# Which expert down products are computed during routing, and where the row steps stand beside them

## The chip, the core and the metric

The kernel runs on one core of a Trainium2 chip. The metric is device time in microseconds (us), the median of several runs. The core has a matrix engine (TensorE, PE in the profile; its weight loads are PEld), VectorE (DVE), ScalarE (ACT), GpSimd (POOL) and SyncE (SP), each with a queue of its own that is worked off in order, and 16 DMA engines that all queues share.

## What is computed

One layer of a trunk: a mixer of three branches, and then an expert layer (PEER) that takes most of the time. 512 tokens, width 2048, all in float32. The part that this case turns on:

```python
def peer_retrieve(h, w_q, sub_keys):                 # 8 heads, 2 x 128 keys, top 16
    q = (h @ w_q).reshape(t, PEER_HEADS, 2, PEER_HALF)
    sc = jnp.einsum('thpc,hpkc->thpk', q, sub_keys)
    top_s, top_i = lax.top_k(sc, PEER_TOPK)
    cand_s = top_s[:, :, 0, :, None] + top_s[:, :, 1, None, :]      # 16 x 16 sums
    best_s, pos = lax.top_k(cand_s, PEER_TOPK)
    idx = jnp.take_along_axis(cand_i, pos, axis=-1)   # expert = 128 * i + j
    return idx, jax.nn.softmax(best_s, axis=-1)

def peer_experts(h, idx, g, w_down, w_up):            # 16384 experts
    a = gelu(einsum('thkd,td->thk', w_down[idx], h))
    return einsum('thk,thkd->td', a * g, w_up[idx])
```

## The kernel before

**Four tiles of 128 tokens, two ways of doing the experts.** Tiles 2 and 3 (`DENSE`, 256 tokens) go densely over all 16384 experts, in 128 blocks of 128. For block `i` there is a *down product* (`down`, L718 to L727): `gelu(h2 @ w_downT[i])`, 128 experts by 256 tokens; it is multiplied by that block's gates out of a matrix `G` (zero nearly everywhere), split, and then an *up product* adds it, times `w_upN`, to the output. Tiles 0 and 1 (`GT` is 1) gather instead: 128 *row steps* for `w_down` and 128 for `w_up`. A row step (`gather`, L817) is an indirect DMA that POOL issues (L829; 128 rows of 8 KB, 1 MB, into one of three buffers `row`) and one DVE pass over 128x2048 (L834 for down, L832 for up).

**Units.** Weights are streamed in units of 512 KB (128x1024), by `halves` (L88), issued on SP. In exact float32 products a unit is split by ACT (`whi`, L112) and DVE (`wlo`, L113) and multiplied in three passes (`mm3`, L118 to L120). With `raw=True` it is not split: plain float32 matmuls (L168), nothing on ACT and DVE, more of PE. A down product takes two units.

**Stages around the change.** `retrieval` finishes tile 0, routes tile 1, and then for the dense tiles does 16 queries (32 units, raw) with top-16 passes on DVE (`tops`), `best` for each tile (the top 16 of the sums), and `dense_gates` (L691): 32 sets for each tile, in a set a mask `B` (L707), four masks `Aw` (L712), four small matmuls `pgd` (L714) and an ACT copy to `gd`; every four sets `gd` is written to DRAM as a part of `G` (`gdram`). Some down products are done *early*, in this stage, raw, by `downs` (L735): `best` calls its argument `fill` five times for two heads' worth of halves (so ten down products a tile), `dense_gates` calls `downs` in every second set (16 a tile). That makes 52, namely blocks 0 to 51, and they are stored in DRAM (`adram`).

`experts` (L868) runs 16 groups of `GI` = 8 blocks. Group `n` runs 16 up units, four for each quarter `c` of the width, 12 matmuls in each (two tiles, two blocks, three passes); after every second unit it calls `first` for one block of group `n+1`: load the stored product from `adram` (if `i < self.n_down`), or compute it with `down` (split, two units); then gates (L885), and the split `aw` (ACT L124, DVE L125). A quarter ends with two additions (L907), a group with eight of them.

**Order.** A scheduler orders each engine's queue by its own estimate, within the dependencies and the edges that the program sets. Row steps are traced by `tick` (L838), which is called after every unit: each call adds 1 to `ticks`, and steps follow until `steps * units < 256 * ticks` no longer holds (`units` is the count of ticks over which the 256 steps are spread). They are queued behind `self.last_lo`, the last split on DVE (L114). Raw units set no `last_lo`, so in the whole of the dense tiles' routing a row step is only held behind a split of the stage before; the scheduler may put it as early as its operands allow.

Of the kernel before, what the change touches and what calls it, by code (L numbers as in the profile page):

```python
# [29 lines left out]
PH = 8  # L30
TOPK = 16
NE = 128
# [7 lines left out]
GI = 8  # L40
# [22 lines left out]
class Builder:  # L63
    def __init__(self, ctx, tc, a):
        self.ctx, self.tc, self.nc, self.a = ctx, tc, tc.nc, a
        self.n_unit, self.n_down, self.extra = 0, 0, (None, 0, 0)
        self.gth, self.last_lo = None, None


    def open(self):  # L70
# [21 lines left out]
    def halves(self, src, raw=False):  # L92


        nc, A = self.nc, self.A
        for u in range(src.shape[-1] // 1024):
            self.n_unit += 1
            if raw:
                tag, bufs = (("raw", 4), ("wlo", 3), ("raw", 4), ("wlo", 3), ("raw", 4), ("wlo", 3), ("raw", 4),
                             ("whi", 3))[self.n_unit % 8]  # L100
                w = A.tile([P, 1024], F32, tag=tag, name="unit", bufs=bufs)
                nc.sync.dma_start(w, src[:, bass.ts(u, 1024)])
                yield (w,)
                continue
            X, nr, ns = self.extra
            pool, b = (X, nr) if self.n_unit % (nr + 4) < nr else (A, 4)
            w = pool.tile([P, 1024], F32, tag="raw", name="raw", bufs=b)
            nc.sync.dma_start(w, src[:, bass.ts(u, 1024)])
            pool, b = (X, ns) if self.n_unit % (ns + 3) < ns else (A, 3)
            hi = pool.tile([P, 1024], F32R, tag="whi", name="whi", bufs=b)  # L110
            lo = pool.tile([P, 1024], F32R, tag="wlo", name="wlo", bufs=b)
            nc.scalar.activation(hi, w, AF.Copy)  # L112
            self.last_lo = nc.vector.tensor_sub(lo, w, hi.bitcast(F32)).ins  # L113
            yield hi, lo  # L114

    def mm3(self, out, lh, ll, rh, rl, start, stop):
        mm = self.nc.tensor.matmul
# [524 lines left out]
    def best(self, t1, i1, bufs, scratch, HH, hh, fill):  # L642
# [5 lines left out]
        full = [P, HH, TOPK, TOPK]  # L648
        three = [P, HH * TOPK, TOPK]
        v.tensor_copy(i1f[:, hs].rearrange("p h s k -> p (h s) k"), i1[:, 2 * HH * hh:2 * HH * (hh + 1)])  # L650
        fill()
        cand = scratch("cand", full)
        v.tensor_tensor(cand, tv[:, hs, 0, :, None].to_broadcast(full), tv[:, hs, 1, None, :].to_broadcast(full),
                        op=ALU.add)
# [36 lines left out]
    def dense_gates(self, d, pick, L):  # L691

        nc = self.nc
        tr = L.tile([P, 3, P], F32, tag="tr", name="tr", bufs=1)
        pt = self.bank("ptr")[:, :3 * P].rearrange("p (s t) -> p s t", s=3)
        for s in range(3):
            nc.tensor.transpose(pt[:, s, :], pick[:, s, :], self.ident)
        nc.scalar.activation(tr, pt, AF.Copy)
        four = [P, 4, P]
        for b in range(P // TB):  # L700
            gd = L.tile([P, NE, TB], F32, tag="gd", name="gd", bufs=2)
            for q in range(TB // 4):
                if q % 2 == 0:
                    self.downs()
                t0 = b * TB + 4 * q
                B = L.tile(four, F32, tag="B", name="B", bufs=2)
                nc.vector.tensor_tensor(B, self.iota[:, None, :].to_broadcast(four),  # L707
                                        tr[:, 1, t0:t0 + 4, None].to_broadcast(four), op=ALU.is_equal)
                A = L.tile(four, F32, tag="Aw", name="Aw", bufs=2)
                pg = self.bank("pgd").rearrange("p (t i) -> p t i", t=4)  # L710
                for z in range(4):
                    nc.vector.tensor_scalar(A[:, z, :], self.iota, tr[:, 0, t0 + z:t0 + z + 1],  # L712
                                            tr[:, 2, t0 + z:t0 + z + 1], op0=ALU.is_equal, op1=ALU.mult)
                    nc.tensor.matmul(pg[:, z], B[:, z, :], A[:, z, :], start=True, stop=True)  # L714
                nc.scalar.activation(gd[:, :, 4 * q:4 * q + 4].rearrange("p i t -> p t i"), pg, AF.Copy)
            nc.sync.dma_start(self.gdram[d * (P // TB) + b], gd.rearrange("p i t -> p (i t)"))
# [12 lines left out]
    def downs(self):  # L729


        i = self.n_down
        ga = self.down(i, True)
        self.nc.sync.dma_start(self.adram[i], ga)
        self.n_down = i + 1  # L735

    def retrieval(self):

# [3 lines left out]
        with tc.tile_pool(name="topk", bufs=1, reuse_waits="tile") as L:  # L742
# [14 lines left out]
            bufs = work()  # L757
# [44 lines left out]
                for c in range(2):  # L802
                    nc.scalar.activation(x[:, bass.ts(c, W)], self.x2[GT][c], AF.Copy)

            self.gathered(take_x, hg, self.weights(bufs), 2 * (2 * PH - len(scores)) + 4 * NE - 28)
            while len(scores) < 2 * PH:
                query()
                tops()
# [29 lines left out]
    def tick(self):  # L838

        g = self.gth  # L840
        if g is None:
            return
        g.ticks += 1
        while g.steps < 2 * P and g.steps * g.units < 2 * P * g.ticks:
            with self.tc.issue_after(self.last_lo):
                self.gather(g)
# [14 lines left out]
    def experts(self):  # L861
        nc, tc, a, A = self.nc, self.tc, self.a, self.A
        gsrc = self.gdram.rearrange("b j (i t) -> j b i t", t=TB)
        self.rpool.close()
        with tc.tile_pool(name="exp", bufs=1, reuse_waits="tile") as L:
            self.extra = L, 0, 1
            aw = {}

            def first(i):
                if i >= NE:  # L870
                    return
                if i % GI == 0:
                    self.gt = L.tile([P, NTB, GI * TB], F32, tag="G", name="G", bufs=2)
                    for b in range(2):
                        bs = slice(b * NTB // 2, (b + 1) * NTB // 2)
                        nc.sync.dma_start(self.gt[:, bs], gsrc[:, bs, i:i + GI, :].rearrange("j b i t -> j b (i t)"))
                if i < self.n_down:
                    ga = L.tile([P, TD], F32, tag="ga", name="ga", bufs=4)
                    nc.sync.dma_start(ga, self.adram[i])
                else:  # L880
# [149 lines left out]
```

## Time and profile before

| what | us |
|---|---|
| median of 3 runs | 3829.25 (3822.52 to 3841.54) |
| the profiled execution | 3832.78 |
| its span, first to last instruction | 3831.0 |
| first dense query on PE | 1948.88 |
| first gate matmul `pgd` | 2183.87 |
| last gate matmul | 2537.1 |
| first up matmul | 2552.97 |
| end of group 15 (last L907) | 3822.2 |

Groups of `experts` are told apart by their eight additions. Groups 1 to 4 (all blocks stored) run from 2606.7 to 2840.9, groups 7 to 12 (all blocks of the next group computed) from 3013.9 to 3584.7, group 14 from 3682.2 to 3773.1. In a row of busy times by stretch, the numbers are us of busy time and, in brackets, instructions; after the engines come the granted share of PE's clock, the busy share of the DMA engines and GB/s. PE's busy times overlap from one matmul to the next (a matmul's end is modelled), so the time that a matmul takes in a full stream is read from start to start.

### The profile page before, as it was taken

The numbers are of one execution on the slowest core, as the hardware profiler recorded it, in microseconds if no ns is written. First come the engines' busy times: TensorE is split into PE (matmuls) and PEld (weight loads), VectorE is DVE, ScalarE is ACT, GpSimd is POOL, SyncE is SP. The second block draws the span as 40 slices with busy tenths as digits, with TensorE's granted clock in tenths as the row PEclk, the third lists the DMA queues.
The fourth block names the chain that finished last, engine by engine and source line by source line (L and its number), as shares of the span: only waits on it lengthen the run. The fifth ranks groups of instructions, "written<-read, shape, count | busy, mean of one in ns | idle before, by whom it ended". The sixth has DMA issues, their size and how long they took to land.

```text
span 3831.0 us, 50500 instructions
## 1 busy us (share of the span) xinstructions
PE 3594.2 (94%) x19270; PEld 3188.1 (83%) x19270; DVE 2984.6 (78%) x3921; ACT 1370.8 (36%) x1793; POOL 676.8 (18%) x544
## 2 busy tenths in 40 slices
PE   9999989899999999999789799988889999999998
PEld 7677778899899999997678688976668888888887
DVE  1588866877888888888799891358878888888886
ACT  1586662332332223233211121233333444434334
POOL 0000000221211232122202220001112222233220
PEclk9999999999999999999999899999999999999999
DMA  7699985789899999999979996579899999999995
GB/s 253 230 357 349 332 328 177 291 335 343 325 337 342 334 356 343 338 350 366 408 286 359 354 367 201 187 242 339 314 326 356 354 371 373 364 367 365 361 346 183
DMA packets 301363, 1236.52 MB, mean 323 GB/s; under 512 B 30912, under 2 KB 76992, under 8 KB 231616
## 3 DMA queue, kind: packets, MB, share of 16 engines
q1 hardware_dynamic: 225520, 689.00, 50.2%
q0 software_dynamic: 73728, 536.90, 36.4%
q10 hardware_dynamic: 1872, 7.39, 0.5%
q8 instruction: 151, 2.47, 0.2%
q14 instruction: 92, 0.75, 0.1%
HBM read 1204.33 MB, written 28.84 MB: 322 GB/s over the span
## 4 chain that ended last, share of the span: by engine, by line
PE 52%; DMA 21%; DVE 17%; issue 6%; ACT 3%; POOL 1%; DVEq 0%; SPq 0%; ACTq 0%; POOLq 0%
DMA raw<-in_w_downT 9%; DMA raw<-in_w_upN 7%; PE pd L168 5%; DVE wlo L113 5%; PE pg L119 4%; PE pg L120 4%; PE pg L118 4%; DMA row<-in_w_down,eidx 3%; DVE row L834 3%; PE pb L119 3%; PE pb L120 3%; PE pb L118 3%; PE po L119 2%; PE pq L168 2%; PE po L120 2%
## 5 line engine op out<-in xcount | busy, mean ns | idle before, releaser
L112 ACT ACTIVATE whi<-raw 128x1024 fp32r<-128x1024 f32 x960 | 999.9, 1058 | 1505.5 <-DMA raw<-in_w_upN 297.8
L113 DVE TENSOR_TENSOR wlo<-raw,whi 128x1024 fp32r<-128x1024 f32 x960 | 1154.7, 1222 | 317.0 <-ACT whi L112 276.7
L832 DVE SCALAR_TENSOR_TENSOR xg<-row,dots,xg 128x2048 f32<-128x2048 f32 x256 | 600.8, 2347 | 30.1 <-DMA row<-in_w_up,eidx 25.3
L834 DVE SCALAR_TENSOR_TENSOR row<-row,hg 128x2048 f32<-128x2048 f32 x256 | 584.7, 2285 | 48.8 <-DMA row<-in_w_down,eidx 48.6
L829 POOL DMA_INDIRECT row<-in_w_down,eidx x256 | 293.3, 1146 | 1622.9 <-DVE row L834 1149.8
L829 POOL DMA_INDIRECT row<-in_w_up,eidx x256 | 368.4, 1439 | 996.6 <-DVE xg L832 899.8
L119 PE MATMUL po<-wlo,aw 128*128 128x512 f32 x1024 | 416.0, 406 | 44.9 <-DVE wlo L113 44.5
L118 PE MATMUL po<-whi,aw 128*128 128x512 f32 x1024 | 405.2, 401 | 48.2 <-ACT whi L112 32.6
L120 PE MATMUL po<-whi,aw 128*128 128x512 f32 x1024 | 408.8, 399 | 0.9 <-DVE aw L125 0.9
L168 PE MATMUL pd<-h,unit 128*128 128x256 f32 x1664 | 368.8, 381 | 7.4 <-DMA unit<-in_w_downT 3.9
L168 PEld LDWEIGHTS pd<-h,unit 128*128 128x128 f32 x1664 | 315.8, 192 | 49.8 <-DMA unit<-in_w_downT 4.3
L120 PE MATMUL pd<-h2h,wlo 128*128 128x256 f32 x1216 | 345.3, 284 | 4.1 <-DVE wlo L113 4.0
L118 PE MATMUL pd<-h2h,whi 128*128 128x256 f32 x1216 | 344.1, 283 | 1.7 <-ACT whi L112 1.7
L119 PE MATMUL pd<-h2l,whi 128*128 128x256 f32 x1216 | 344.2, 283 | 0.0
L119 PEld LDWEIGHTS po<-wlo,aw 128*128 128x128 f32 x1024 | 198.0, 193 | 105.3 <-DVE wlo L113 67.1
L118 PEld LDWEIGHTS po<-whi,aw 128*128 128x128 f32 x1024 | 198.1, 194 | 95.0 <-ACT whi L112 39.2
L118 PE MATMUL pg<-hiT,whi 128*128 128x384 f32 x768 | 262.0, 341 | 2.0 <-ACT whi L112 2.0
L120 PE MATMUL pg<-hiT,wlo 128*128 128x384 f32 x768 | 261.4, 340 | 0.0
L119 PE MATMUL pg<-loT,whi 128*128 128x384 f32 x768 | 261.0, 340 | 0.0
L120 PEld LDWEIGHTS pd<-h2h,wlo 128*128 128x128 f32 x1216 | 233.1, 192 | 5.9 <-DVE wlo L113 5.8
L118 PEld LDWEIGHTS pd<-h2h,whi 128*128 128x128 f32 x1216 | 233.1, 192 | 5.2 <-ACT whi L112 2.3
L119 PEld LDWEIGHTS pd<-h2l,whi 128*128 128x128 f32 x1216 | 233.1, 192 | 2.9
(356 smaller groups left out, 5948.0 us busy)
## 6 DMA issues: line engine op xcount, KB each, us to landing
raw<-in_w_upN SPq DMA_DIRECT2D x256, 512.0 KB, 6.9
raw<-in_w_restN SPq DMA_DIRECT2D x176, 512.0 KB, 6.1
raw<-in_w_rest SPq DMA_DIRECT2D x176, 512.0 KB, 7.1
raw<-in_w_downT SPq DMA_DIRECT2D x152, 512.0 KB, 8.1
unit<-in_w_downT SPq DMA_DIRECT2D x104, 512.0 KB, 5.1
unit<-in_w_q SPq DMA_DIRECT2D x96, 512.0 KB, 6.4
raw<-in_w_out SPq DMA_DIRECT2D x72, 512.0 KB, 7.1
raw<-in_w_branchN SPq DMA_DIRECT2D x48, 512.0 KB, 6.0
```

The costliest lines, as they stand in the source:

```text
L112: nc.scalar.activation(hi, w, AF.Copy)
L113: self.last_lo = nc.vector.tensor_sub(lo, w, hi.bitcast(F32)).ins
L118: mm(out, lh, rh, start=start, stop=False)
L119: mm(out, lh, rl, start=False, stop=False)
L120: mm(out, ll, rh, start=False, stop=stop)
L168: self.nc.tensor.matmul(out, parts[0][:, k, :], act.raw(kk), start=first, stop=last)
L829: nc.gpsimd.indirect_dma_start(out=row, out_offset=None, in_=self.a["w_up" if up else "w_down"], in_offset=bass.IndirectOffsetOnAxis(ap=g. ...
L832: nc.vector.scalar_tensor_tensor(g.x, row, g.dots[:, k:k + 1], g.x, op0=ALU.mult, op1=ALU.add)
L834: nc.vector.scalar_tensor_tensor(row, row, 1.0, g.hg, op0=ALU.mult, op1=ALU.mult, accum_out=g.dots[:, k:k + 1])
```

## The change

The early down products are 38 instead of 52. They are no longer blocks 0 to 51 but chosen over groups 1 to 15: of every group the blocks 3 and 6, and of every odd group also block 0 (30 and 8). `fill` loses its first call in `best` (four calls where there were five, so eight down products a tile and one query less in tile 1's half), `dense_gates` calls `downs` in every third set (11 a tile). Blocks 0 to 7, and five or six of each later group, are computed split in `experts`; `first` asks `self.stored`.

Row steps: a raw unit now sets `last_lo` to the last DVE instruction traced so far, so that the scheduler can't pull a step ahead of what was traced before it. A tick counts 1.4 in routing and 1 in `experts`, and `units` follows.

```diff
+        self.early = [i for i in range(GI, NE) if i % GI in (3, 6) or i % (2 * GI) == GI]
+        self.stored = set()
@@ halves, raw
                 w = A.tile([P, 1024], F32, tag=tag, name="unit", bufs=bufs)
+                self.last_lo = self.last_of(nc.vector) or self.last_lo
                 nc.sync.dma_start(w, src[:, bass.ts(u, 1024)])
@@
+    def last_of(self, engine):
+        return next((i for i in reversed(self.nc.cur_bb.bb.instructions) if i.engine == engine.engine), None)
@@ best
         v.tensor_copy(i1f[:, hs].rearrange("p h s k -> p (h s) k"), i1[:, 2 * HH * hh:2 * HH * (hh + 1)])
-        fill()
         cand = scratch("cand", full)
@@ dense_gates
-                if q % 2 == 0:
+                if (4 * b + q) % 3 == 0:
                     self.downs()
@@ downs
-        i = self.n_down
-        ga = self.down(i, True)
-        self.nc.sync.dma_start(self.adram[i], ga)
-        self.n_down = i + 1
+        if self.early:
+            i = self.early.pop(0)
+            self.nc.sync.dma_start(self.adram[i], self.down(i, True))
+            self.stored.add(i)
@@ retrieval
-            self.gathered(take_x, hg, self.weights(bufs), 2 * (2 * PH - len(scores)) + 4 * NE - 28)
+            self.gathered(take_x, hg, self.weights(bufs), 0)
+            self.pace = 1.4
+            before = 2 * (2 * PH - len(scores)) + 2 * len(self.early)
+            self.gth.units = self.pace * before + 4 * NE - 2 * len(self.early) - 28
@@ tick
-        g.ticks += 1
+        g.ticks += self.pace
@@ experts
         self.rpool.close()
+        self.pace = 1.0
@@ first
-                if i < self.n_down:
+                if i in self.stored:
```

What moves on the engines is shown at three places. `hg1` is tile 1's scaled input, `dots` its products, `tr` the routing of one dense tile (its number tells the tile).

DVE, in the gates. Before, from the 25th of the first dense tile's 32 sets on; 40 sets of both tiles follow the row step below, and one more row step stands among them, behind the 36th.

```order
L834 SCALAR_TENSOR_TENSOR row_18539,dots_15627<-row_18539,hg1_15437 128x2048
L707 TENSOR_TENSOR B_17165<-iota_75,tr_16483 128x512
L712 TENSOR_SCALAR Aw_17167<-iota_75,tr_16483 128x128 x4
L707 TENSOR_TENSOR B_17178<-iota_75,tr_16483 128x512
L712 TENSOR_SCALAR Aw_17180<-iota_75,tr_16483 128x128 x4
L707 TENSOR_TENSOR B_17218<-iota_75,tr_16483 128x512
```

After, at the border of the two tiles' gates; eleven row steps stand together there, the last two of them are shown:

```order
L843 SCALAR_TENSOR_TENSOR row_17487,dots_15600<-row_17487,hg1_15437 128x2048
L843 SCALAR_TENSOR_TENSOR row_17536,dots_15600<-row_17536,hg1_15437 128x2048
L713 TENSOR_TENSOR B_17542<-iota_75,tr_17508 128x512
L718 TENSOR_SCALAR Aw_17544<-iota_75,tr_17508 128x128 x4
L713 TENSOR_TENSOR B_17555<-iota_75,tr_17508 128x512
L718 TENSOR_SCALAR Aw_17557<-iota_75,tr_17508 128x128 x4
L713 TENSOR_TENSOR B_17568<-iota_75,tr_17508 128x512
L718 TENSOR_SCALAR Aw_17570<-iota_75,tr_17508 128x128 x4
L843 SCALAR_TENSOR_TENSOR row_17602,dots_15600<-row_17602,hg1_15437 128x2048
```

Counted on DVE's queue from tile 1's routing (L566) on: before, 44 row steps stand ahead of the first gate mask, 21 among the gates and 1 between these and the first L885; now 28 ahead, 14 among the first tile's gates, 11 at the border, 13 among the second tile's, 3 after it.

PE, at the end of the gates. Before, the up products follow the last gate matmuls:

```order
L714 MATMUL pgd_18571<-Aw_18570,B_18568 128x128 x4
L118 MATMUL po_18638<-whi_18642,aw_18593 128x512
L119 MATMUL po_18638<-wlo_18643,aw_18593 128x512
L120 MATMUL po_18638<-whi_18642,aw_18593 128x512
L118 MATMUL po_18638<-whi_18642,aw_18599 128x512
```

After, the down product of block 0 does, and seven more:

```order
L720 MATMUL pgd_18241<-Aw_18240,B_18238 128x128 x4
L125 MATMUL pd_18260<-h2h_13772,whi_18263 128x256
L126 MATMUL pd_18260<-h2l_13773,whi_18263 128x256
L127 MATMUL pd_18260<-h2h_13772,wlo_18264 128x256
L125 MATMUL pd_18260<-h2h_13772,whi_18263 128x256
```

ACT, in the early groups of `experts`. Before, the split `aw` of a stored product stands alone among the splits of the up units:

```order
L124 ACTIVATE aw<-ga 128x256
L112 ACTIVATE whi<-raw 128x1024 x2
L124 ACTIVATE aw<-ga 128x256
L112 ACTIVATE whi<-raw 128x1024
L124 ACTIVATE aw<-ga 128x256
L112 ACTIVATE whi<-raw 128x1024 x3
```

After, computed products (the gelu `ga<-pd`) come in every group, and a stored one's `aw` mostly stands beside that of a computed one:

```order
L131 ACTIVATE aw<-ga 128x256
L116 ACTIVATE whi<-raw 128x1024 x4
L732 ACTIVATE ga<-pd 128x256
L131 ACTIVATE aw<-ga 128x256 x2
L116 ACTIVATE whi<-raw 128x1024 x6
L732 ACTIVATE ga<-pd 128x256
```

## Rows read from the trace of the kernel before

**Rows 1.** The page's head.

```profile
span 3831.0 us, 50500 instructions
```

**Rows 2.** Busy time by stretch, from routing to the end; columns in the first row.

```profile
core 0: us, PE busy (x) PEld busy (x) DVE busy (x) ACT busy (x) POOL busy (x), PEclk, DMA share, GB/s
1949.00:2184.00 235.00, 202.73 (x933) 173.87 (x931) 212.93 (x579) 25.64 (x60) 55.34 (x47) 0.95 0.90 347
2184.00:2300.00 116.00, 109.11 (x573) 97.37 (x574) 106.91 (x219) 31.48 (x38) 26.74 (x21) 0.97 0.92 349
2300.00:2537.00 237.00, 237.00 (x1255) 213.00 (x1254) 71.58 (x197) 52.55 (x73) 0.98 (x2) 1.00 0.58 190
2537.00:2553.00 16.00, 0.40 (x5) 0.21 (x3) 2.04 (x4) 2.78 (x5) 0.89 (x1) 0.68 0.92 299
...
2606.70:2840.90 234.20, 194.25 (x771) 149.44 (x769) 187.71 (x225) 77.78 (x97) 35.18 (x32) 0.94 0.91 328
...
3013.90:3584.70 570.80, 550.70 (x3453) 496.25 (x3453) 504.58 (x435) 231.82 (x288) 166.12 (x97) 0.99 0.97 366
...
3682.20:3773.10 90.90, 85.87 (x534) 76.25 (x533) 70.74 (x67) 39.47 (x49) 12.35 (x7) 1.00 0.79 280
3773.10:3831.00 57.90, 48.38 (x233) 40.53 (x231) 34.54 (x53) 24.96 (x45) 0.00 (x0) 0.96 0.47 163
```

**Rows 3.** PE in order of time, gates with raw down products: start, length, instructions.

```profile
2406.80 7.07 PE L168 MATMUL pd<-h,unit 128*128 128x256 f32 x32
2413.71 1.95 PE L714 MATMUL pgd<-Aw,B 128*128 128x128 f32 x16
2415.49 7.07 PE L168 MATMUL pd<-h,unit 128*128 128x256 f32 x32
```

**Rows 4.** PE in order of time, group 8: two up units, then a down unit.

```profile
3110.43 0.40 PE L118 MATMUL po<-whi,aw 128*128 128x512 f32 x1
...
3115.90 0.28 PE L118 MATMUL pd<-h2h,whi 128*128 128x256 f32 x1
...
3118.77 0.28 PE L118 MATMUL pd<-h2h,whi 128*128 128x256 f32 x1
```

**Rows 5.** PE in order of time, the first gate matmuls.

```profile
2183.87 3.75 PE L714 MATMUL pgd<-Aw,B 128*128 128x128 f32 x16 [17.00 <-DVE Aw L712]
```

**Rows 6.** DVE by line, 1949 to 2184 (first row) and 2184 to 2300.

```profile
L834 DVE SCALAR_TENSOR_TENSOR row<-row,hg 128x2048 f32<-128x2048 f32 x44 | 100.5, 2285 | 21.6 <-DMA row<-in_w_down,eidx 21.5
...
L834 DVE SCALAR_TENSOR_TENSOR row<-row,hg 128x2048 f32<-128x2048 f32 x20 | 45.5, 2284 | 8.1 <-DMA row<-in_w_down,eidx 8.1
L712 DVE TENSOR_SCALAR Aw<-iota,tr 128x128 f32<-128x128 f32 x102 | 28.3, 348 | 0.0
L707 DVE TENSOR_TENSOR B<-iota,tr 128x512 f32<-128x512 f32 x25 | 17.1, 683 | 0.0
```

**Rows 7.** Splits L113 on DVE, one a unit: groups 1 to 4, 7 to 12.

```profile
2606.70:2840.90 234.20, 78.36 (x65) 0.94 0.91 328
...
3013.90:3584.70 570.80, 231.21 (x192) 0.99 0.97 366
```

**Rows 8.** Row steps, same stretches: DVE, then POOL, one a step.

```profile
2606.70:2840.90 234.20, 73.33 (x64) 35.18 (x32) 0.94 0.91 328
...
3013.90:3584.70 570.80, 227.58 (x98) 166.12 (x97) 0.99 0.97 366
```

**Rows 9.** By line: DVE and ACT in groups 1 to 4; last, groups 7 to 12.

```profile
L907 DVE TENSOR_TENSOR x<-x,po 128x512 f32<-128x512 f32 x32 | 21.6, 683 | 5.7 <-PE po L120 5.4
L125 DVE TENSOR_TENSOR aw<-ga,aw 128x256 fp32r<-128x256 f32 x32 | 13.5, 422 | 40.8 <-ACT aw L124 40.8
L885 DVE TENSOR_TENSOR ga<-ga,G 128x256 f32<-128x256 f32 x32 | 13.4, 418 | 0.0
...
L112 ACT ACTIVATE whi<-raw 128x1024 fp32r<-128x1024 f32 x65 | 68.9, 1060 | 155.1 <-DMA raw<-in_w_upN 122.4 <-PE po L120 32.7
...
L125 DVE TENSOR_TENSOR aw<-ga,aw 128x256 fp32r<-128x256 f32 x48 | 20.1, 419 | 0.9 <-ACT aw L124 0.9
```

More of the change, by code (lines that the diff above doesn't have):

```diff
@@ L65, in __init__ @@
         self.ctx, self.tc, self.nc, self.a = ctx, tc, tc.nc, a
-        self.n_unit, self.n_down, self.extra = 0, 0, (None, 0, 0)
-        self.gth, self.last_lo = None, None
+        self.n_unit, self.extra = 0, (None, 0, 0)
+        self.gth, self.last_lo, self.pace = None, None, 1.0
+        self.early = [i for i in range(GI, NE) if i % GI in (3, 6) or i % (2 * GI) == GI]
+        self.stored = set()
     def open(self):
```

## The prediction

> **What bounds the kernel now.** I read the span [rows 1], then busy times by stretch [rows 2], to see which engine is full where, then within each stretch what one piece of work takes and what its engine waits for. Up to 1949 us the two programs do the same work in the same order; all that follows is about 1949 to 3831. Two stretches carry the argument, and both leave something empty.
>
> The end of routing, 2300 to 2537: PE is busy for all of 237 us, while DVE works 71.6 and the DMA engines are at 0.58 [rows 2]. PE runs raw down products there, back to back: 32 matmuls in 2413.71 - 2406.80 = 6.91 us, then 16 gate matmuls in 1.78 [rows 3]. Nothing waits for these products; they are only early. Just before, 1949 to 2184, it is the other way: DVE is busy 213 of 235 us, 44 row steps among it, and PE stands 17.0 us before the first gates, waiting for a mask of DVE [rows 2, 5, 6].
>
> The groups of experts come in two kinds. Count them by units, one DVE split each. Groups 1 to 4, with all products stored, take 234.2 / 65 = 3.60 us a unit; groups 7 to 12, with all computed, 570.8 / 192 = 2.97 [rows 7]. PE needs nearly the same in both: 24 matmuls of an up unit pair start over 5.47 us, so 2.73 a unit, and 24 of a down unit over 2.87 [rows 4]. So the computed kind is close to PE's own rate (half of each: 2.80 of 2.97), and the stored kind is not. What holds the stored kind: DVE is busy 187.7 / 65 = 2.89 a unit and otherwise waits, 40.8 us of it at L125, for ACT's half of the same split (32 times 1.27 us); ACT sits in order behind splits that wait 122.4 us for a DMA [rows 9]. In the computed kind that wait is 0.9 us in all [rows 9].
>
> **The change part by part.**
>
> *Fourteen raw down products fewer in routing.* 14 x 6.91 = 96.7 us of PE [rows 3]. In the last 237 us that is on the path one for one. PE's need over the stage falls from 52 x 6.91 + 32 x 1.78 (gates) + 16 x 6.91 (queries, the same matmul) = 527 to 430 us, of 588.
>
> *Row steps kept in place.* Ahead of the first gate mask stand 28 instead of 44. Each is 2.29 us of DVE and 21.6 / 44 = 0.49 of waiting for its rows [rows 6]: 16 x 2.78 = 44.5, so the first gates come after 235 - 44.5 = 190.5 us. PE needs 16 queries and 8 down products by then, 166 us, and is still the one that waits. From there DVE has what it had after 2184 without rows: 106.9 + 71.6 - 45.5 (20 rows) - 4.6 (two) - 3.7 (three splits) = 124.7 [rows 2, 6]; a set of masks is 17.1 / 25 + 4 x 28.3 / 102 = 1.8, so 32 sets 57.6 [rows 6]. First tile's gates: 124.7 - 57.6 + 14 rows x 2.78 = 106 on DVE, 11 x 6.91 + 16 x 1.78 = 104.5 on PE. Border: eight down products, 55.3 on PE, cover the eleven rows (25 to 31 on DVE). Second tile: 57.6 + 13 x 2.78 = 94 on DVE, 104.5 on PE. With no friction that is 190.5 + 106 + 55.3 + 104.5 = 457; with the idle time that PE has now (588 - 527 = 61), 430 + 61 = 491. DVE, PE and the DMA engines (some 95 MB in the last 280 us, at 349 GB/s [rows 2] 272) are all near full, so I take 470, 13 us of friction: **-118**, bounds -97 and -131. Each row step also issues 1 MB on POOL; POOL has nothing else queued, and its steps keep their order. On SP the weights are queued behind `gd` writes as before, ten units ahead.
>
> *Eight down products at the start of experts*, blocks 0 to 7, no longer stored. 16 units; PE needs 8 x 5.74 = 46, and no up unit can start before. At 3.0 a unit (below): **+48**. They hide the 16 us in which PE now waits for the first `aw` [rows 2]: **-16**.
>
> *Groups 0 to 13.* 16 up units each and 77 computed products in all, 378 units; now they take 3682.2 - 2553 = 1129.2 us. The price of a unit is the unknown. Below: 2.97, the computed kind's. PE's need is 2.79 here; rows are 0.467 a tick for 97 / 192 = 0.505 [rows 7, 8], which takes 0.04 x 2.3 = 0.09 us off DVE; gates and additions are 8 for 27 units instead of 8 for 32, which adds 0.05 x 1.52 = 0.07 [rows 9]; so DVE's load per unit is that of the computed kind (504.6 / 192 = 2.63). Above: straight between the kinds by gates per unit (0.25 at 2.97, 0.5 at 3.60, here 0.297), 3.09; that is also what comes out if each of the 38 stored products keeps its 1.27 us wait. On ACT a stored `aw` now stands beside that of a computed one, as where the wait is 0.9, so I stay near the lower end: 3.0, 1134 us, **+5**. A lower price than 2.97 has one reason, a rival below.
>
> *Group 14.* 90.9 us for 32 units [rows 2], with hardly any rows: 2.84 a unit. It has 26 now, 73.8: **-17**. Group 15 and the tail, 57.9 [rows 2], stay.
>
> *The bytes.* 14 MB more weights in experts, 3 MB fewer rows, 2 MB fewer loads of stored products. At 366 GB/s [rows 2] all that experts move would take some 1255 us of about 1313 from the last gate on, so the DMA engines don't set the end, though closely. Loads from `adram` fall from 52 to 38, stores too; both lie beside PE's work.
>
> **How PE's fill is read.** By matmul busy time the stored kind is at 0.83 and the computed one at 0.96; by weight loads 0.64 and 0.87 [rows 2]. The Trainium skill's page "Perfetto Trace Analysis", section "Identifying the Most-Contended Engine", says that matmul busy time is not a good measure of how near PE is to its limit, and to use MFU and weight-load busy time instead. By weight loads the stored kind's price would fall from 3.60 to 2.64, below what PE needs for an up unit here, and the sum would be some 140 us lower; by matmul busy time to 3.09, 35 higher. Neither is used: a down unit has twice the loads of an up unit in the same time, so here the share of loads tells the mix, and start to start [rows 4] tells the need.
>
> **The sum.** -118 + 48 - 16 + 5 - 17 = -98: span 3831 - 98 = 3733. The profiled execution took 1.8 us more than its span and lies 3.5 above the median of the runs, so 3731; I say 3732.
>
> **The rivals.**
> 1. *Mixing gives nothing*: stored products keep their wait wherever they stand, 3.09. For it: the wait is one of order between two engines, and the order stays in-order. 394 units x 0.09 = +35: 3767. Chance 0.18.
> 2. *Better than the computed kind*: fewer rows and spread loads give group 14's 2.84 throughout. Against it: group 14 has nearly no rows. 394 x 0.16 = -63: 3669. Chance 0.08.
> 3. *The gates become the bound*: rows now stand ahead of masks that PE waits for, and each pays a full landing instead of 0.49 us. The 1949 stretch moved 347 GB/s with its rows [rows 2]; if a row in the gates costs 2.29 + 3 (about one row's 1 MB at that rate), 38 rows x 2.5 = +95: 3827, no change. Against it: three buffers, and 20 rows in the gates of before waited 8.1 us in all [rows 6]. Chance 0.06.
> 4. *Slower*: what holds the stored kind is in truth the mixture of 1 MB rows and unit loads on the DMA engines, and more computed units among them don't cure it, so all 394 units cost up to 3.60: +236, 3968. It decides at 3.0 + (98 + 19) / 394 = 3.30, from which the kernel is slower by over 0.5%. Against it: the computed kind has as many rows a unit and moves 366 GB/s to the stored kind's 328. Chance 0.04.
> 5. *The steps don't move*: the order of the queues shows that they do. 0.01.
>
> **How the numbers follow.** My forecast has 0.63. 0.5%, 19 us, is about what a measurement of this kernel can tell from no change. Faster by more: the forecast, rivals 1 and 2, 0.89. Within: most of rival 3 and the tails, 0.06. Slower: rival 4 and half of a rest, 0.05. The range runs from the lower bound of routing (-13) with a price of 2.90 (-39), 3680, to rival 1 with routing's upper bound (+21), 3788.
>
> **What would show it.** Right: the last gate matmul near 2419, the first up near 2467; in the gates DVE and PE both above 90% and no stretch with DVE at a third; groups 1 to 13 alike, near 80 us each with PE's clock at 0.98 or more; waits at L125 of a few us in all. Routing ending after 2450 would make its term wrong (look at PE's waits for `Aw`, and at DVE's for rows); groups of 84 us would be rival 1. It would all be wrong if the groups' rate went to 300 GB/s with PE waiting for units.

## The result, and the profile after

The changed kernel takes 3731.7 us (median, 3724.9 to 3737.7); the kernel before, beside it on the same chip, 3827.4. The ratio is 0.974, 95% interval 0.971 to 0.978: faster, and at the predicted 3732. The size is right. One of the two reasons for it was wrong, and most of the experiments are about that one.

The profiled execution is 3737.7 us, 6 above the median, and its span 3736.0. First the busy times by stretch, to be laid beside [rows 2]: routing of the dense tiles up to the first gate matmul; the first tile's gates; the border; the second tile's gates; the eight down products of group 0; then two groups of experts, one that computes six down products meanwhile and one that computes five; groups 0 to 13 together; group 14; the end.

```profile
core 0: us, PE busy (x) PEld busy (x) DVE busy (x) ACT busy (x) POOL busy (x), PEclk, DMA share, GB/s
1946.90:2144.20 197.30, 186.51 (x870) 160.45 (x869) 185.11 (x560) 24.59 (x57) 39.92 (x31) 0.98 0.86 321
2144.20:2251.90 107.70, 101.73 (x578) 90.27 (x577) 101.29 (x230) 38.16 (x45) 20.92 (x15) 0.98 0.87 314
2251.90:2314.30 62.40, 62.40 (x293) 54.91 (x292) 25.27 (x30) 4.63 (x11) 13.24 (x11) 1.00 0.93 366
2314.30:2413.20 98.90, 98.75 (x579) 89.03 (x577) 83.60 (x181) 38.54 (x45) 19.07 (x13) 1.00 0.84 309
2413.20:2465.80 52.60, 48.17 (x386) 47.97 (x385) 38.40 (x46) 21.27 (x31) 7.75 (x8) 0.94 1.01 376
2540.30:2625.40 85.10, 80.59 (x482) 71.52 (x481) 71.90 (x80) 32.80 (x41) 16.88 (x13) 0.98 0.93 342
2625.40:2702.90 77.50, 73.31 (x427) 63.65 (x426) 66.69 (x74) 32.22 (x40) 16.44 (x12) 1.00 0.97 361
2465.80:3607.80 1142.00, 1086.75 (x6375) 962.98 (x6375) 978.45 (x946) 455.62 (x570) 284.62 (x177) 0.98 0.95 352
3607.80:3678.20 70.40, 69.51 (x405) 61.17 (x404) 53.71 (x54) 31.92 (x40) 3.82 (x3) 1.00 0.81 283
3678.20:3736.00 57.80, 48.52 (x234) 40.67 (x232) 34.54 (x53) 25.10 (x45) 0.00 (x0) 0.96 0.47 163
```

Where [rows 2] had a stretch of 237 us with DVE at 0.30 and the DMA engines at 0.58, the gates now have DVE busy for 101.3 of 107.7 us in the first tile and 83.6 of 98.9 in the second, and the DMA engines at 0.84 to 0.93. The prediction's sign, DVE and PE both above 90%, holds in the first tile alone: in the second DVE is at 0.85, at the border at 0.40. Routing takes 2413.2 - 1946.9 = 466.3 us, before it was 588. The two moments that the prediction named stand on PE's timeline (start, length, instructions): the last gates end at 2413.2, the first up product starts at 2465.8, right behind a down product.

```profile
2411.74 1.50 PE L720 MATMUL pgd<-Aw,B 128*128 128x128 f32 x12
...
2465.64 0.28 PE L127 MATMUL pd<-h2h,wlo 128*128 128x256 f32 x1
2465.76 0.40 PE L125 MATMUL po<-whi,aw 128*128 128x512 f32 x1
```

And a wait that the kernel before did not have. DVE by line in groups 1 to 12, 2540.3 to 3525.3 (busy, mean ns, idle before and what ended it; L895 is the gate product, L885 before):

```profile
L117 DVE TENSOR_TENSOR wlo<-raw,whi 128x1024 fp32r<-128x1024 f32 x325 | 391.0, 1220 | 76.6 <-ACT whi L116 75.3 <-PE po L127 0.8
...
L895 DVE TENSOR_TENSOR ga<-ga,G 128x256 f32<-128x256 f32 x96 | 39.6, 419 | 66.6 <-DMA G<-gdram 42.1 <-ACT ga L732 12.9 <-DMA ga<-adram 11.6
L132 DVE TENSOR_TENSOR aw<-ga,aw 128x256 fp32r<-128x256 f32 x96 | 37.8, 420 | 2.4 <-ACT aw L131 2.4
```

The wait for ACT's half is down from 40.8 us in four groups [rows 9] to 2.4 in twelve, as predicted. But DVE stands 42.1 us before gate products, until the load of a later group's `G` has landed. The waits of one group (3355.7 to 3444.6; engine, line, awaited: us, times, longest) show how it goes on from there:

```profile
DVE wlo L117 <- ACT whi L116: 7.8, 6, 3.1
DVE ga L895 <- DMA G<-gdram: 7.2, 1, 7.2
...
PE pd L127 <- DVE wlo L117: 4.4, 2, 2.9
```

DVE's queue shows why: the scheduler has put the gate product of a *stored* block, which waits for nothing but two loads, far ahead; of the 128 gate products, 38 stand ahead of one of an earlier group. Here block `ga_19888` of the next group (`G_19554`) stands in front of the splits of the group at hand (`G_18858`):

```
L895 TENSOR_TENSOR ga_18970<-ga_18970,G_18858 128x256
L117 TENSOR_TENSOR wlo_19056<-raw_19053,whi_19055 128x1024
L132 TENSOR_TENSOR aw_18973<-ga_18970,aw_18973 128x256
L895 TENSOR_TENSOR ga_19888<-ga_19888,G_19554 128x256
L117 TENSOR_TENSOR wlo_19092<-raw_19089,whi_19091 128x1024
L843 SCALAR_TENSOR_TENSOR row_19107,dots_15600<-row_19107,hg1_15437 128x2048
```

At this first place `G` had landed in time, and DVE did not stand (the product starts at 2493.94, without idle time before it). In the group of the waits above it had not, and everything behind on DVE waited along: a split that starts at 3377.29 stands behind two gate products, which stood for 7.25 us.

```profile
3368.14 1.22 DVE L117 TENSOR_TENSOR wlo<-raw,whi 128x1024 fp32r<-128x1024 f32 x1 [0.95 <-ACT whi L116]
3376.61 0.76 DVE L895 TENSOR_TENSOR ga<-ga,G 128x256 f32<-128x256 f32 x2 [7.25 <-DMA G<-gdram]
3377.29 1.22 DVE L117 TENSOR_TENSOR wlo<-raw,whi 128x1024 fp32r<-128x1024 f32 x1
```

### The profile page after: what moved, and what is told of

It is laid out like the page before. It is cut to its first block, busy times and chain, and to the rows that moved or that the text cites. A ratio compares the mean times of both kernels' runs of the same rounds, so it can differ in the third digit from the quotient of the medians.

```text
span 3736.0 us, 51012 instructions
## 1 busy us (share of the span) xinstructions
PE 3565.5 (95%) x19494; PEld 3186.2 (85%) x19494; DVE 3014.3 (81%) x3949; ACT 1397.1 (37%) x1821; POOL 695.2 (19%) x544
## 4 chain that ended last, share of the span: by engine, by line
PE 57%; DMA 20%; DVE 13%; issue 6%; ACT 3%; POOL 0%; SPq 0%; DVEq 0%; ACTq 0%; POOLq 0%
DMA raw<-in_w_upN 8%; DVE wlo L117 6%; PE pd L175 5%; PE pq L175 5%; PE pg L126 4%; PE pg L127 4%; PE pg L125 4%; DMA raw<-in_w_downT 4%; PE pb L126 3%; PE pb L127 3%; PE pb L125 3%; PE po L126 2%; PE po L127 2%; PE po L125 2%; DMA G<-gdram 2%
## 5 line engine op out<-in xcount | busy, mean ns | idle before, releaser
L116 ACT ACTIVATE whi<-raw 128x1024 fp32r<-128x1024 f32 x988 | 1026.9, 1057 | 1452.9 <-PE pg L126 281.0
L117 DVE TENSOR_TENSOR wlo<-raw,whi 128x1024 fp32r<-128x1024 f32 x988 | 1186.7, 1220 | 336.7 <-ACT whi L116 295.1
L127 PE MATMUL pd<-h2h,wlo 128*128 128x256 f32 x1440 | 416.7, 289 | 24.9 <-DVE wlo L117 24.4
L125 PE MATMUL pd<-h2h,whi 128*128 128x256 f32 x1440 | 414.5, 288 | 10.0 <-ACT whi L116 9.8
L126 PE MATMUL pd<-h2l,whi 128*128 128x256 f32 x1440 | 413.9, 287 | 0.0
L125 PE MATMUL po<-whi,aw 128*128 128x512 f32 x1024 | 402.2, 393 | 0.6 <-ACT whi L116 0.6
L127 PEld LDWEIGHTS pd<-h2h,wlo 128*128 128x128 f32 x1440 | 282.8, 196 | 29.5 <-DVE wlo L117 29.4
L125 PEld LDWEIGHTS pd<-h2h,whi 128*128 128x128 f32 x1440 | 282.7, 196 | 15.0 <-ACT whi L116 11.9
L126 PEld LDWEIGHTS pd<-h2l,whi 128*128 128x128 f32 x1440 | 282.8, 196 | 3.1
L175 PE MATMUL pd<-h,unit 128*128 128x256 f32 x1216 | 272.7, 381 | 4.6 <-DMA unit<-in_w_downT 4.6
L125 PE MATMUL pg<-hiT,whi 128*128 128x384 f32 x768 | 262.1, 341 | 2.0 <-ACT whi L116 2.0
L175 PEld LDWEIGHTS pd<-h,unit 128*128 128x128 f32 x1216 | 228.9, 191 | 34.4 <-DMA unit<-in_w_downT 5.0
```

Source lines behind the costliest of these rows:

```text
L125: mm(out, lh, rh, start=start, stop=False)
L126: mm(out, lh, rl, start=False, stop=False)
L127: mm(out, ll, rh, start=False, stop=stop)
L175: self.nc.tensor.matmul(out, parts[0][:, k, :], act.raw(kk), start=first, stop=last)
```

## The experiments

Two theories of the gain stood at the start. *Mine*: row steps in the gates let routing shrink by what PE no longer does, and mixing stored with computed products brings a unit of the stored kind from 3.60 to 3.0 us, since the wait for ACT at L125 goes. *The rival*: the mixing gives nothing, and routing alone is the gain. The first five runs take the change apart. Routing (first dense query to last gate) and the rest (last gate to end of span) are from PE's timelines of the profiled executions, the totals are medians:

| kernel | early products | steps pinned | routing | rest | total | ratio to before |
|---|---|---|---|---|---|---|
| before | 52, blocks 0 to 51 | no | 588 | 1294 | 3827 | 1 |
| `e1_count` | 38, blocks 0 to 37 | no | 488 | 1356 | 3793 | 0.991 (0.988 to 0.993) |
| `e2_spread` | 52, spread | no | 590 | 1252 | 3794 | 0.991 (0.989 to 0.993) |
| `e3_rows` | 52, blocks 0 to 51 | yes, pace 1.4 | 550 | 1263 | 3753 | 0.980 (0.978 to 0.982) |
| `e4_unpinned` | 38, spread | no | 480 | 1335 | 3760 | 0.981 (0.979 to 0.984) |
| `e5_contig` | 38, blocks 0 to 37 | yes, pace 1.4 | 467 | 1325 | 3737 | 0.975 (0.973 to 0.977) |
| after | 38, spread | yes, pace 1.4 | 466 | 1323 | 3732 | 0.974 (0.971 to 0.978) |

**`e1_count`: only fewer products.** Against after:

```diff
-        self.early = [i for i in range(GI, NE) if i % GI in (3, 6) or i % (2 * GI) == GI]
+        self.early = list(range(38))
-                self.last_lo = self.last_of(nc.vector) or self.last_lo
-            self.pace = 1.4
+            self.pace = 1.0
```

> Only the count changes: 38 early down products, blocks 0 to 37, 8 a tile in best and 11 in the gates; row steps are not pinned and a tick counts 1, as before. My theory (routing gives back its raw products one for one, but the groups without computed products stay at 3.60 us a unit): routing ends some 90 us earlier, experts computes 14 products more at about 4.5 us each over what a stored one costs, +63; about -30 against before, 3797. Rival (the count alone is what the change is worth, spread and rows do nothing): 3731, as the changed kernel.

It came out at 3792.6. Routing falls by 100 us, the 96.7 of the fourteen products and a little more; experts give back 62.

**`e2_spread`: only the spread**, 52 products at `i % GI in (1, 3, 6) or (i % (2 * GI) == 0 and i)`, five in routing for each `best` again, steps not pinned.

> Only the places change: 52 early down products as before, but spread over groups 1 to 15 (of each group blocks 1, 3 and 6, and block 0 of groups 2, 4 to 14), so blocks 0 to 7 are computed first; row steps not pinned. My theory (an even mix runs near the computed kind's price): routing as before, +48 for the first eight, -16 for the wait before the first up product, and 376 units of groups 0 to 14 at 3.0 to 3.05 us instead of 392 units in 1220 us: -75 to -90; about -50, 3777. Rival (mixing gives nothing, 3.11 a unit): about -18, 3809.

3794.3, between the two numbers. Routing does not move (590), and the stored kind's price is gone: groups 0 to 14 take 1141.4 us for 376 units, 3.04 each. Before, groups 1 to 4 took 3.60 [rows 7], and groups 0 to 14 together 1220.1 / 392 = 3.11. So rival 1 falls in its strict form, but the price came down a little less than to 3.0.

**`e3_rows`: only the steps**, with 52 products in their old blocks and places.

> Only the row steps change: pinned behind the last DVE instruction traced, a tick counts 1.4 in routing; 52 early down products, blocks 0 to 51, as before. My theory: 16 row steps leave the stretch ahead of the first gates, which comes 40 us earlier; after that PE's raw products bind and nothing else is lost: -35 to -45, about 3787. Rival (the steps only move from one side of the gates to the other; the masks wait for rows and PE for the masks): within 10 us of before.

3753.1, 34 us better than I expected. Routing falls by 38, which was expected. The rest falls by 31, and this I had missed: at pace 1.4 and with 52 products (more ticks in routing), 83 row steps stand ahead of the last gate mask, where before has 65 and after 66. Eighteen fewer behind it go with 31 us, 1.7 each. That is an average: groups 1 to 4 fall by 14.9 us, to 219.3, while groups 7 to 12, with nine rows fewer among them, do not fall at all (571.7, before 570.8).

**`e4_unpinned` and `e5_contig`: the change without the steps, and without the spread.**

```diff
 e4
-                self.last_lo = self.last_of(nc.vector) or self.last_lo
-            self.pace = 1.4
+            self.pace = 1.0
 e5
-        self.early = [i for i in range(GI, NE) if i % GI in (3, 6) or i % (2 * GI) == GI]
+        self.early = list(range(38))
```

> The changed kernel without its row part: 38 products spread over the groups, but row steps not pinned and a tick counts 1. My theory: the first gates come at 235 us after the first dense query again instead of 197, and PE's 265 us of gates and products follow, so routing is 30 to 40 us longer than in the changed kernel: 3760 to 3772. Rival (with only 38 products DVE's row steps are hidden wherever they stand): 3732, as the changed kernel.

> The changed kernel without the spread: count 38 and the row part as changed, but the early products are blocks 0 to 37. My theory: routing as in the changed kernel (last gate 465 us after the first dense query), then groups 1 and 2 at about 57 us, the later ones at 94 as in the kernel of count alone, and the 16 us before the first up product back: experts 1325 to 1335 from the last gate on, about 3760 in all, 25 to 30 slower than the changed kernel. Rival (where the computed products stand does not matter): 3732.

Without the steps 3760.2, as expected, some 28 us over after. Without the spread 3736.5, within 5 us of after, as the rival had it. So in the change as it was made the spread gives nothing that these runs can tell. Two things work against my price there. The stored kind is cheaper in this kernel: of `e5_contig` the first row below is groups 1 and 2 (all stored, 32 units, 3.43 each), the second group 4 (computed, 2.97):

```profile
2475.60:2585.40 109.80, 95.16 (x387) 73.61 (x385) 90.36 (x110) 39.78 (x49) 15.73 (x15) 0.95 0.93 334
2650.60:2745.70 95.10, 92.83 (x593) 83.80 (x591) 80.64 (x87) 37.61 (x47) 18.53 (x15) 1.00 0.96 358
```

The same two groups take 116.6 us in `e1_count`, with 17 rows fetched and not 15. That the two rows are the reason is not shown: 6.8 us for two is more than any price of a row found below, as are the 14.9 us of `e3_rows` in groups 1 to 4 for three (29, before 32). And the spread brings the new wait for `G`, which eats its gain. That was tried next.

**`e7_pingate`: after, with a stored block's gate product queued behind the last split.**

```diff
-                nc.vector.tensor_mul(gv, gv, g)
+                if i in self.stored and i >= GI:
+                    with tc.issue_after(self.last_lo):
+                        nc.vector.tensor_mul(gv, gv, g)
+                else:
+                    nc.vector.tensor_mul(gv, gv, g)
```

> The changed kernel with one edit: the gate product of a stored block (L895) is queued behind the last DVE split traced, so that it is not pulled ahead of the splits of earlier units while its G is still on its way. In the changed kernel groups that compute six products take 3.08 us a unit, those with five 2.96, and DVE waits 42 us in twelve groups for G. My theory (that wait on DVE delays the splits and PE): seven groups of 28 units at 2.96, -20 to -25, 3708. Rival (the wait lies beside PE's work): within 6 us of the changed kernel.

3710.4 (ratio to before 0.967, 0.965 to 0.970), 21 us better than after. Routing is the same, 466; groups 0 to 13 fall from 1142.0 to 1118.7 us, 2.96 a unit. DVE by line in groups 1 to 12; L897 is the gate product of a stored block, L899 of a computed one:

```profile
L117 DVE TENSOR_TENSOR wlo<-raw,whi 128x1024 fp32r<-128x1024 f32 x325 | 392.4, 1221 | 103.9 <-ACT whi L116 99.9 <-PE pd L126 3.1
...
L899 DVE TENSOR_TENSOR ga<-ga,G 128x256 f32<-128x256 f32 x66 | 27.6, 418 | 11.5 <-ACT ga L732 11.5
L897 DVE TENSOR_TENSOR ga<-ga,G 128x256 f32<-128x256 f32 x30 | 12.5, 416 | 0.0
```

The 42.1 us are gone, and so are 11.6 before loads of stored products. Not all of it was lost time: 24.6 come back as waits for ACT's half of a split (75.3 to 99.9), and the groups fall by 23.3. Beside `e5_contig`, 3736.5, the spread without its wait is worth 26 us, as I had expected of it there.

**`e6_hi_dve`: does the wait for ACT set the stored kind's price?** The kernel before, with both halves of a stored product's split on DVE, so that it waits for ACT no more.

```diff
-                self.split(w[:, 0, :], w[:, 1, :], ga)
+                if i < self.n_down:
+                    nc.vector.tensor_copy(w[:, 0, :], ga)
+                    nc.vector.tensor_sub(w[:, 1, :], ga, w[:, 0, :].bitcast(F32))
+                else:
+                    self.split(w[:, 0, :], w[:, 1, :], ga)
```

> The kernel before with one edit: for a stored product the upper half of the split aw is made by DVE (a copy that rounds, about 0.42 us more of DVE) instead of ACT, so that DVE has no wait for ACT at the lower half. My theory of the stored kind's price (DVE waits 1.27 us for ACT, 52 times): groups 1 to 4 from 58.5 to about 52 us, in all 52 x (1.27 - 0.42) = -44, 3785. Rival (the stored kind's price comes from 1 MB rows and units mixed on the DMA engines): groups 1 to 4 not faster, 0 to +22, 3829 to 3851.

3843.0, ratio 1.003 (1.001 to 1.005): no gain. Groups 1 to 4 take 59.3 us each, before 58.6. My mechanism falls. Their waits show where the 40.8 us went:

```profile
ACT whi L112 <- DMA raw<-in_w_upN: 124.5, 47, 9.2
PEld po L118 <- ACT whi L112: 40.8, 11, 7.1
DVE x L911 <- PE po L120: 40.7, 11, 9.5
```

DVE now waits 40.7 us for PE, PE for ACT's half of a unit, and ACT for the unit itself, 124.5 us, as before [rows 9]. The wait at L125 was the last link of a chain that leads to late units. It need not begin at the DMA engines: SP, which issues the units (L108), waits in the same groups of before for buffers that DVE frees.

```profile
SPq L108 <- DVE wlo L113: 65.0, 38, 4.2
...
SPq L108 <- DVE aw L125: 36.4, 11, 6.3
SPq L108 <- DVE ga L885: 32.8, 12, 3.9
```

What makes units late there? Three more runs leave work out of the kernel before and are read in groups 1 to 4 (`e9_noload` leaves out the loads of every stored block from 8 on).

**`e9_noload`, `e10_nofetch`, `e12_shortop`: what makes the units late.**

```diff
 e9, at the load of a stored product
-                    nc.sync.dma_start(ga, self.adram[i])
+                    if i < GI:
+                        nc.sync.dma_start(ga, self.adram[i])
 e10, in gather
+        bare = not up and 1 <= self.group <= 4
+        if not bare:
             nc.gpsimd.indirect_dma_start(out=row, ...
-            nc.vector.scalar_tensor_tensor(row, row, 1.0, g.hg, ...
+            nc.vector.scalar_tensor_tensor(row, g.hg if bare else row, 1.0, g.hg, ...
 e12, in gather
+            n = 64 if 1 <= self.group <= 4 else D
-            nc.vector.scalar_tensor_tensor(row, row, 1.0, g.hg, ...
+            nc.vector.scalar_tensor_tensor(row[:, :n], row[:, :n], 1.0, g.hg[:, :n], ...
```

> The kernel before, but from group 1 of experts on a stored product is not loaded: its gate product reads one fixed tile instead (work left out: the outputs of those blocks are wrong). Question: what makes a unit of the all-stored groups 1 to 4 cost 3.60 us, after the DVE split showed that the wait for ACT's half does not. Theory A, order on SP: the load of a stored product waits on SP's queue for its buffer, which DVE frees (42.3 us in 16 waits in 2606.7 to 2840.9), the unit loads behind it start late, and ACT waits 122.4 us for raw units. Then groups 1 to 4 fall from 58.6 to about 50 us each and the run to about 3780. Theory B, 1 MB row loads and units share the DMA engines: groups 1 to 4 stay above 55.5 (the bytes left out, 32 x 128 KB at 328 GB/s, are 12.8 us in all, 3.2 a group, at the most) and the run stays at 3812 to 3835. Theory C, DVE's own queue with its row operations: stays as in B.

> The kernel before, but in groups 1 to 4 of experts the row steps fetch no row: DVE's operation of the same size reads a fixed tile (work left out: 33 rows of tile 1, so its output is wrong); stored products are loaded as before. Theory A (order on SP): groups 1 to 4 stay at 56 to 58.6 each, run 3820 to 3835. Theory B (row loads of 1 MB and units share the DMA engines; 34.6 of the 77.2 MB in the stretch are rows): units land in time, ACT's wait for them falls from 122 us to under 40, groups 1 to 4 fall to 48 to 50 each, run about 3790 to 3795. Theory C (DVE's queue, its row operations standing in front of splits): nothing changes, 58.

> The kernel before, but in groups 1 to 4 of experts the row steps fetch their rows as before while DVE's operation takes 64 columns of 2048 (work left out: most of those rows' products, so the output of tile 1 is wrong). Leaving out the fetches brought these groups from 58.6 to 49.1 us; this tells whether the fetches alone make units late, or only together with a DVE that has no room. Theory D, both: DVE's need falls from 2.89 to about (187.7 - 33 x 2.2) / 65 = 1.77 us a unit, late units are caught up, and groups 1 to 4 fall to 46 to 51 us, as the computed kind, which carries as many rows a unit, lets one expect; run 3790 to 3800. Theory E, the DMA engines alone: units land as late as before, groups 1 to 4 stay at 56 to 59, run 3820 to 3835. In between (51 to 56): each has a part.

Groups 1 to 4 of the three, in that order (columns as above; before: 234.2 us, DVE 187.7, DMA 0.91, 328 GB/s [rows 2]):

```profile
2606.40:2835.50 229.10, 190.66 (x760) 146.49 (x761) 187.50 (x226) 78.04 (x97) 35.22 (x33) 0.96 0.88 314
```

```profile
2605.60:2802.00 196.40, 179.56 (x764) 141.28 (x763) 186.03 (x226) 78.89 (x97) 2.82 (x3) 1.00 0.71 225
```

```profile
2604.80:2836.30 231.50, 192.56 (x783) 154.15 (x782) 128.30 (x237) 80.29 (x102) 36.98 (x33) 0.93 0.93 345
```

Without the stored products' loads a group takes 57.3 us, so the order of loads on SP is not it (theory A). Without the row fetches, and with DVE doing the same work, it takes 49.1: the fetches are 9.5 of 58.6 us, and DVE, at 186 of 196 us, is then nearly full. That is theory B's number. With the fetches, but DVE's need cut to 128 us, a group takes 57.9, theory E's number. But this third run does not decide between D and E. Two lines of its waits:

```profile
ACT whi L112 <- DMA raw<-in_w_upN: 88.1, 38, 5.2
DVE ga L886 <- DMA ga<-adram: 62.4, 16, 9.3
```

ACT waits less for units than before (122.4 us [rows 9], now 88.1), and DVE has a wait that it did not have: 62.4 us before gate products, for the loads of stored products, where before has 0 [rows 9]. With short row operations the scheduler has moved these gate products ahead, up to four in a row, and the splits stand behind them, as behind `G` above. The group with most of that wait, 26.4 us, is the slowest, 71.2 us; the other three take 55.0, 54.8 and 50.5. So it is shown that the row fetches hold these groups back, by 9.5 us each. Whether they do so on the DMA engines alone (E), or only beside a DVE with little room, which frees the buffers of units late (D), stays open. One line of the waits goes with the fetches, the one my mechanism was built on, in `e10_nofetch`:

```profile
DVE aw L125 <- ACT aw L124: 9.0, 10, 2.8
```

40.8 us before, 9.0 when nothing but fetches is left out. One number of theory B was missed: ACT's wait for raw units falls only to 91.7 us, not under 40; SP still waits there for buffers that DVE frees, 134.8 us of 196.4 before loads of units (L108). The totals are of one run each: 3813.6, 3798.8 and 3818.9, against 3835.6, 3835.6 and 3826.2 of before beside them. In `e10_nofetch` the four groups (-37.8) account for all of it; in `e9_noload` for 5 of 22, and where the other 17 lie, a few us each in other groups, was not followed up.

Also open: a unit of the stored kind moves 77.2 MB / 65 = 1.19 MB (the trace's DMA view of these groups), 9% more than 209.2 / 192 = 1.09 of the computed kind, which at 366 GB/s would be 3.25 us and not 3.60. Why the DMA engines reach 328 GB/s in the one and 366 in the other at a busy share of 0.91 and 0.97 was not settled. A kernel with more buffers for units was not tried.

**`e8_pace18` and `e11_pin18`: more steps ahead of experts.** If rows are dear in experts, more of them belong in routing. Pace 1.8 puts 14 more ahead of the last gate mask (80, after 66; the 69 of the first expectation counts on to the first gate product); once on after, once on `e7_pingate`.

```diff
-            self.pace = 1.4
+            self.pace = 1.8
```

> The changed kernel with one number: a tick counts 1.8 in routing instead of 1.4, which puts 80 row steps ahead of experts instead of 69 (33 ahead of the first gate mask instead of 28). From the rows alone (18 steps fewer in experts were worth 32 us there): experts -18 to -20; routing +5 to +14, since five more steps stand ahead of the first gates; about -8, 3724. Rival (routing has no room: DVE and the DMA engines are full in its gates, each step costs its 2.8 us): +10, 3742.

> The kernel after with both edits that helped: the gate product of a stored block queued behind the last split, and pace 1.8 (14 more row steps ahead of experts). If both gains add up: 3731.7 - 21.3 - 4.3 = about 3706; if row steps out of experts are worth as much as in pace 1.8 alone (19 us) and routing grows by 10: 3701. Rival: with the waits for G gone DVE has room, rows in experts cost less, and moving them to routing is a loss: 3715 to 3721, slower than the queued version alone (3710.4).

3727.4 alone (ratio 0.972, 0.969 to 0.974; routing +10, rest -19), not to be told from after. On `e7_pingate` 3691.9 (ratio 0.963, 0.961 to 0.965), some 18 us better than `e7_pingate` and the fastest of all, 9 to 14 us below both of my numbers. Routing costs 8 more, the rest is 28 shorter, 2.0 us a row. Groups 0 to 13 of it:

```profile
2475.70:3561.70 1086.00, 1065.77 (x6363) 947.49 (x6362) 951.14 (x922) 456.46 (x570) 277.83 (x164) 1.00 0.97 358
```

2.87 a unit with PE busy 98% of the time. This is nearly the bound that the prediction gave for rival 2 (2.84).

## Why the prediction was right, point by point

Term by term against the sum:

| term | predicted | measured |
|---|---|---|
| up to the first dense query | 1949 | 1946.9 |
| routing | 470 (457 to 491) | 466.3 |
| first eight down products | 48 | 52.6 |
| gap before the first up product | 0 | 0 |
| groups 0 to 13 | 1134 (3.0 a unit) | 1142.0 (3.02) |
| group 14 | 73.8 | 70.4 |
| group 15 and the tail | 57.9 | 57.8 |
| span | 3733 | 3736.0 |

**Routing: right, and for the reason given.** The four stretches were to be 190.5, 106, 55.3 and 104.5 us and 13 of friction; they are 197.3, 107.7, 62.4 and 98.9. In all the gates (2144.2 to 2413.2) PE waits 5.8 us for masks, and DVE 21.9 for rows, so rival 3 (gates bound by landings) fell:

```profile
DVE row L843 <- DMA row<-in_w_down,eidx: 21.9, 10, 5.6
...
PE pgd L720 <- DVE Aw L718: 5.8, 5, 4.6
```

The mechanism is shown apart: fewer products alone give 100 us (`e1_count`), steps in place alone 38 (`e3_rows`).

**Row steps: right in routing, mis-sized in experts.** Of their place in experts the prediction counted only DVE's 2.3 us, "0.09 us off DVE" a unit. They cost time on the path there: 14 to 18 fewer gave 1.4 (`e8_pace18`), 1.7 (`e3_rows`) and 2.0 us each (`e11_pin18`). That this is their DMA and not their DVE work is not shown for the mixed groups. After has 66 of them ahead of the last gate mask and 3 more ahead of the first gate product, before 65 and 1, so this moved next to nothing in the sum; at another pace it would have.

**The price of a unit: the right number by a wrong step, which is luck.** The step that failed is "What holds the stored kind: DVE is busy 187.7 / 65 = 2.89 a unit and otherwise waits, 40.8 us of it at L125, for ACT's half of the same split". That wait was a symptom: moving the split off ACT changed nothing (`e6_hi_dve`), taking the row fetches away took both it and the price (`e10_nofetch`). The line that spoke of it stood in the same group: ACT, the one waited for, itself waited 122.4 us for a DMA [rows 9], and I read that as background. Rival 4 named the rows beside the units at a chance of 0.04, and its argument against held: the computed kind carries as many rows and moves 366 GB/s. So the rows were the cause in the stored groups before, and its consequence, all units at 3.60, did not come. Why the mix with its rows runs near the computed kind's price is not shown.

**3.0 a unit then was two errors that cancel.** Without the new wait for `G` the groups cost 2.96 (`e7_pingate`), about the 2.97 that I gave as the lower bound; with it 3.02. Nothing in the profile of before shows that wait, since there no gate product of a later group stands ahead of one of an earlier. But the order of the changed kernel showed it, and I looked there for the splits on ACT and not for what a stored product's gate waits for on DVE.

**The parts do not add up.** Alone, count, spread and steps give 37, 35 and 76 us, 148 in all; together 96. By the table about 15 us of the difference lie in routing (100 and 38 alone, 122 together: after the count the steps give 14, 480 to 466) and about 40 in the rest (+62, -42 and -31 alone, +29 together). The wait for `G`, without which the rest is 25 shorter (`e7_pingate`), is a part of the 40. That spread and steps cure the same groups, and each leaves less for the other, is argued and not shown.

**How PE's fill is read.** The Trainium skill's page "Perfetto Trace Analysis" ("Identifying the Most-Contended Engine") would have PE's fill read from MFU and weight-load busy time. By weight loads the prediction priced the stored kind at 2.64 us a unit. The trace does not bear that out here: the least that groups 0 to 13 of any of these kernels reached is 2.87 (`e11_pin18`), and there PE's matmuls are busy 1065.8 of 1086.0 us while its weight loads are at 947.5, 0.87.

## What to carry to other kernels

A wait between two engines is a price only if its far end does not wait itself: follow the one waited for to the end of the chain before moving work off it, and test by taking the far end away. An operation that depends on loads alone can be pulled ahead by a scheduler that orders by its own estimate, and on an in-order queue it holds everything behind it (`e12_shortop` fell into this too, so a run that leaves work out needs its waits read before its time is believed); queue it behind the work it belongs to. When large fetches and a stream of weights share the DMA engines, try the fetches where these stand idle; here 14 rows moved so gave 18 us on `e7_pingate`, and on after nothing that can be told.

## What was unexpected of the hardware

A fetched row of 1 MB costs about (234.2 - 196.4) / 32 = 1.2 us in groups 1 to 4 with DVE's operation kept (`e10_nofetch`). Its bytes take 2.9 us at 366 GB/s, so by this estimate more than half of its transfer still lies beside other work. And the DMA engines can do more than the 366 GB/s of the groups: at the border of the gates, with 14 row fetches and raw units only, `e11_pin18` has

```profile
2256.50:2318.90 62.40, 62.40 (x293) 54.91 (x292) 35.70 (x40) 4.63 (x11) 15.89 (x14) 1.00 1.02 416
```

416 GB/s over 62 us, while PE is never idle. (The Trainium skill's page "Perfetto Trace Analysis", section "Roofline", has about 435 GB/s for the 16 DMA engines of a core that is active alone; this stretch comes within 5% of it, the groups of experts, at 366, stay 16% below.) The prediction used 366 as the rate of the experts' stream, and rated the DMA engines as close but not the bound. Which of two engines at 0.95 and 0.97 busy is the bound, busy shares do not tell; in the mixed groups no run left work out, so there it stays open.
